# A decoder layer on one core: the token products in another order, the layer norm beside them, and the memory weights loaded from elsewhere

## The chip, the cores and the metric

The kernel runs on one core of a Trainium2 chip. A core has five engines that work side by side, each on a list of instructions of its own, in order: TensorE (PE in the profile; matmuls and transposes), VectorE (DVE), ScalarE (ACT), GpSimd (POOL) and SyncE (SP, which here only issues transfers). Semaphores tie the lists together. The on-chip memory SBUF feeds the engines, matmuls add up in the banks of PSUM, and 16 DMA engines move data to and from the chip's main memory. The metric is device time in microseconds (us) for one execution, less is better.

## The reference

One layer of a decoder for 1024 tokens of width 1024, in fp32: a gated FFN, a mixer of three branches, and a second FFN. The change lies in the mixer:

```python
h = rmsnorm(x, mix_norm[l])
z = h @ w_in[l]                       # u | v | c_q | c_kv | k_rope | q_mem | gates
u = gelu(z[..., COL_U:COL_V]); v = gelu(z[..., COL_V:COL_CQ])
y_a = spatial_gating(u, v, ...)       # u * (tril(W_s) layernorm(v) + b), 8 chunks of 128, 8 groups
y_b = mla(c_q, c_kv, k_rope, ...)     # low-rank q, k, v; norms; rotary; causal attention
y_c = memory_attention(q_mem, mem, ...)   # 4 heads, keys and values from 256 memory rows
merged = sum(sigmoid(gate_i) * (y_i @ w_branch_i))
x = x + merged @ w_out[l]
```

## The kernel before

Every fp32 product is computed as three matmuls on a rounded part and a rest (`mm3`: hi·hi, lo·hi, hi·lo). The two parts are made by `split`: ScalarE casts the rounded part, VectorE subtracts it to get the rest. Names that end in `hi` and `lo` are such pairs; `h`, `x`, `w`, `raw` are room of shared pools.

The kernel is one straight program. Who does what when is set in two ways: by the order in which the code is written, from which a scheduler makes one list for each engine, and by `after(i, first)` (L403), which holds instruction i behind another one in its engine's list and makes no semaphore wait of its own. Transfers take eight semaphores in turn, so an issue also waits until the transfer eight places before it has landed.

The stretch around the change, in the profile's time:

- **Token products** (`token_rows`, 988 to 1060 us): the columns of z that hold half of v and the low-rank latents of q, k and v are made for all tokens by a scheme of seven products (`b11`, `t2`, `b21`, `t1`, `t3`, `b22`, `t4`), each on halves of the rows, the inner width and the columns. Sums of products give half 0 (tokens 0 to 511) and half 1. `lat.norm` normalises a half's latents, `lat.turn` transposes them on TensorE. Here half 1 is done first.
- **q/k/v stage** (`qkv`, 1060 to 1110 on TensorE): four iterations of two tiles of 128 tokens, in the order 4, 6, 0, 2. TensorE multiplies, ScalarE copies out of PSUM (q L451, squares L452 and L462, k L463, v L464), VectorE sums and scales (L453 to L482), GpSimd rotates q (`rotate`, L358 to L363), and SyncE stores v, k and q to main memory (`vd` L467, `kd` L487, `qd` L490). Between iterations the generator `asides` does something else: the second turn, memory rows, and the layer norm of half 0.
- **Spatial gating and memory products** (`sgu`, 1110 to 1158): `mem_kv` makes keys and values from the memory rows in two products of 48 matmuls, with weights (`wkv`) that `mem_weights` loads as hi/lo pairs; `head_norm` normalises the keys (squares and copies L624, L625, reductions L626, product L630); `layer_norm` (statistics L551, L552, then L555 and L557) finishes v; `split(0)` and `split(1)` round its halves to `v_hi`, `v_lo` (L134, L135); a table load and a small `warm` activation (L603) prepare the later exponentials; `mix(0)` and `mix(1)` are the gating's matmuls, eight copies `u` each (L587), transposes (L593) and the product with u's transpose (L594), whose result `t` is split to `x`, the input of the first branch product. `branches` casts the branch weights from `raw` to `whi`, `wlo`. The tiles `v_hi` and `v_lo` lie in a pool of their own, in the room that q, k and v of the stage before have left, so their first writer waits for the last stores from there.
- After this come the branch products, memory attention and causal attention, the output product and the second FFN. The change doesn't touch these.

Of the kernel before, what the change touches and what calls it, by code (L numbers as in the profile page):

```python
# [8 lines left out]
F32 = mybir.dt.float32  # L9
F32R = mybir.dt.float32r  # L10
# [6 lines left out]
P = 128  # L17
D = 1024
# [31 lines left out]
class Kernel:  # L50
# [3 lines left out]
    def __init__(self, ctx, tc, a, out):  # L54
        self.tc, self.nc, self.a, self.out, self.last = tc, tc.nc, a, out, None
# [77 lines left out]
    def split(self, hi, lo, src, eng=None):  # L133
        self.nc.scalar.copy(hi, src)  # L134
        return (eng or self.nc.vector).tensor_tensor(lo, src, hi.bitcast(F32), op=ALU.subtract)  # L135
# [292 lines left out]
    def qkv(self, lat, asides):  # L428
# [8 lines left out]
        with tc.tile_pool(name="qkvp", bufs=2) as p:  # L437
            for i0 in (4, 6, 0, 2):
                q = p.tile([P, T, H, QK], F32, name="q")
# [3 lines left out]
                for t in range(T):  # L443
# [19 lines left out]
                    nc.scalar.copy(k[:, t, :, :NOPE], pv[:, :, :NOPE])  # L463
                    nc.scalar.copy(v[:, t], pv[:, :, NOPE:])  # L464
                    nc.vector.tensor_reduce(ss[:, 1, t], sq, axis=AXX, op=ALU.add)
                    nc.vector.tensor_scalar(ss[:, 1, t], ss[:, 1, t], krs[:, i:i + 1], None, op0=ALU.add)
                nc.sync.dma_start(self.vd[:, i0:i0 + T], v.rearrange("p t h d -> p t (h d)"))  # L467
                var = self.stat("qk_v", 2 * T * H)
                v4 = var.rearrange("p (a t h) -> p a t h", a=2, t=T)
                for t in range(T):  # L470
# [10 lines left out]
                    k[:, :, :, :NOPE], k[:, :, :, :NOPE], bk.to_broadcast([P, T, H, NOPE]), op=ALU.mult)  # L481
                nc.vector.tensor_tensor(  # L482
                    k[:, :, :, NOPE:], krr[:, i0:i0 + T].unsqueeze(2).to_broadcast([P, T, H, ROPE]),
# [4 lines left out]
                for t in range(T):  # L488
                    d = self.qd[:, :, i0 + t].rearrange("g p e -> p g e")
                    nc.sync.dma_start(d, q[:, t].rearrange("p (g x) d -> p g (x d)", x=2))  # L490
                next(asides, None)

# [51 lines left out]

    def layer_norm(self, v):

        nc = self.nc
        st = self.small.tile([P, 2, 6], F32, name="bn", tag="bn")
        mv = self.small.tile([P, 2, 2], F32, name="mv", tag="mv")
        for k in range(2):  # L550
            nc.vector.bn_stats(st[:, k], v[:, k])  # L551
            nc.vector.bn_aggr(mv[:, k], st[:, k])  # L552
        r = self.rms(mv[:, :, 1], 2, 1)
        for k in range(2):
            nc.vector.scalar_tensor_tensor(  # L555
                v[:, k], in0=v[:, k], scalar=mv[:, k, 0:1], in1=self.ln[:, 0], op0=ALU.subtract, op1=ALU.mult)
            nc.vector.scalar_tensor_tensor(  # L557
                v[:, k], in0=v[:, k], scalar=r[:, k:k + 1], in1=self.ln[:, 1], op0=ALU.mult, op1=ALU.add)

    def sgu(self, rows, p, sink):  # L560
        nc, a, tc = self.nc, self.a, self.tc
        v8 = lambda tag, dt=F32R: p.tile([P, 4, SGW], dt, name=tag, tag=tag, bufs=2)
        if True:
# [10 lines left out]
            def split(hf):  # L574
                vs[hf] = v8("v_hi"), v8("v_lo")
                for i, v in enumerate(rows[hf]):
                    self.split(*(x[:, 2 * i:2 * i + 2] for x in vs[hf]), v)

# [21 lines left out]
            for v in rows[1]:  # L600
                self.layer_norm(v)
            split(1)
            nc.scalar.activation(self.stat("warm", 1), vs[1][0][:, 3, SGW - 1:].bitcast(F32), ACT.Exp, scale=0.0)  # L603
            mix(0)
# [128 lines left out]
    def mem_kv(self, mt, w):  # L733


        nc, a = self.nc, self.a
        kt, vv = (tuple(self.h4(F32R) for _ in range(2)) for _ in range(2))
        kt = tuple(t.rearrange("p a (b m) -> p (a b) m", b=2) for t in kt)

        def product(w):  # L740
# [9 lines left out]
        self.head_norm(x, [ps[:, 0], ps[:, 1]])  # L750
        w = self.mem_weights(1, [None] * 4)
        yield
# [233 lines left out]
    def mixer(self, lat):  # L986
# [17 lines left out]
        with tc.tile_pool(name="lt", bufs=1) as p:  # L1004
            half = ROPE // 2
            for hf in (1, 0):
                t = slice(hf * 4, hf * 4 + 4)
# [504 lines left out]
class Gates(Seven):  # L1512
# [87 lines left out]
    def token_rows(self):  # L1600
# [41 lines left out]
        w = ready(S2)  # L1642
        p1, low = room(h4)
        for t in range(4):
            nc.scalar.copy(p1[t], a[t][:, :RW])
        lat.gain()
        product(x, w, "t2", True)
        w = ready(A12)
        both(A12, A12, S2, ALU.subtract)
        v1, _ = room(w4)  # L1650
        for t in range(4):
            tt(v1[t], p1[t], x[t][:, :RW], op=ALU.add)
        both(A21, A21, A22, ALU.add)
# [9 lines left out]
        v2, _ = room(w4)  # L1663
        for t in range(4):
            tt(v2[t], p1[t], x[t][:, :RW], op=ALU.add)
        lat.norm(1, high)
        y = [k.bank() for _ in range(4)]
        product(y, w, "t3", True)
        w = ready(A12)
        lat.v[0] = [h4() for _ in range(2)]  # L1670
# [12 lines left out]
        k.ln = h4()  # L1683
        for n, name in enumerate(("sg_ln_g", "sg_ln_b")):
            nc.sync.dma_start(k.ln[:, n], k.a[name].partition_broadcast(P))
        product(y, w, "t4", ps=(1,))
        for t in range(4):
            tt(v1[t], v1[t], y[t][:, :RW], op=ALU.add)
            gelu(1, t, v1[t], False)
        return lat  # L1690


class Latents:


    def __init__(self, k, src):
        self.k, self.src, self.v, self.xs = k, src, {}, {}
        self.krs, self.eps, self.cs = (k.const.tile([P, NT], F32, name=n) for n in ("krs", "eps", "cs"))
# [8 lines left out]
    def norm(self, half, ts):  # L1707
# [11 lines left out]
        for n, x in enumerate(xs):  # L1719
            nc.vector.scalar_tensor_tensor(  # L1720
                x[:, :KVR], in0=x[:, :KVR], scalar=r[:, n:n + 1], in1=self.g, op0=ALU.mult, op1=ALU.mult)
# [14 lines left out]
    def turn(self, half, bank=None):  # L1736

        k, xs = self.k, self.xs.pop(half)
        if half:
            self.ckv = [k.split_pair(k.h4) for _ in range(2)]  # L1740
            self.cq.append(k.split_pair(k.h4))
# [433 lines left out]
```

## Time and profile before

| | |
|---|---|
| median of 3 runs | 2191.41 us (2190.87 to 2194.07) |
| the profiled execution's own time | 2190.79 us |
| its span | 2189.1 us |
| granted clock of TensorE, mean | 0.996 |
| PE busy | 2164.3 us, 99% of the span |
| DVE, ACT, POOL busy | 72%, 42%, 13% |
| DMA | 329.97 MB, 151 GB/s over the span |

A share of 99% leaves some 25 us in which TensorE does nothing. The views that matter here are those that name a stretch: windows (busy time of every engine between two times), waits (what ended an engine's idle time) and the timeline (instructions one by one). A time is the distance from the span's start. A matmul's duration in the timeline overlaps the next one's; the distance of two starts is what it costs.

### The profile page before, as it was taken

Reading aid. Unit: us, or ns where it says so; the run is one execution under the profiler, and the core shown is the slowest. Engines: PE = TensorE matmul, PEld = TensorE weight load, DVE = VectorE, ACT = ScalarE, POOL = GpSimd, SP = SyncE. Lnnn points to the kernel's source line nnn. Section 1 sums busy time; section 2 is a strip of 40 time slices with the busy share of each in tenths; the row PEclk is TensorE's granted clock in tenths of the full one; section 3 lists DMA queues with packets and bytes.
Section 4 is the critical chain, followed back from the end, with each engine's and each line's share of the span. In section 5 each row is a group of like instructions: output and inputs, shape, how many; then the busy total and the mean of one; then the engine's idle time right before and its main releaser. Section 6 shows DMA issues by size and latency. Waiting matters only on the chain.

```text
span 2189.1 us, 27495 instructions
## 1 busy us (share of the span) xinstructions
PE 2164.3 (99%) x10154; PEld 1806.3 (83%) x10154; DVE 1583.6 (72%) x2389; ACT 915.2 (42%) x1500; POOL 275.4 (13%) x274
## 2 busy tenths in 40 slices
PE   9999999999999999999989999999999999999999
PEld 5888888888887888888968889988888888888887
DVE  7976666679889656755876679885886666667884
ACT  5433333343455434434545459833432322234332
POOL 2011111100000000000232321140011211210000
PEclk9999999999999999999989999999999999999999
DMA  4253444485432455542576631093033223338443
GB/s 146 92 192 139 146 140 144 151 308 169 134 118 97 144 173 178 198 137 92 173 269 232 247 147 59 13 347 142 29 137 98 102 97 102 115 124 294 169 130 106
DMA packets 125367, 329.97 MB, mean 151 GB/s; under 512 B 14768, under 2 KB 23088, under 8 KB 125232
## 3 DMA queue, kind: packets, MB, share of 16 engines
q1 hardware_dynamic: 125232, 328.21, 43.0%
q8 instruction: 80, 1.31, 0.2%
q14 instruction: 55, 0.45, 0.1%
HBM read 223.82 MB, written 104.33 MB: 150 GB/s over the span
## 4 chain that ended last, share of the span: by engine, by line
PE 90%; DVE 5%; ACT 2%; DMA 1%; issue 1%; POOL 1%; SPq 0%; ACTq 0%; POOLq 0%; DVEq 0%
PE one L151 15%; PE one L152 15%; PE one L153 15%; PE bank L151 13%; PE bank L152 12%; PE bank L153 12%; PE bank L926 1%; PE mm L151 1%; PE mm L152 1%; PE mm L153 1%; PE bank L941 1%; PE bank L942 1%; PE bank L421 1%; DVE wlo L140 1%; DMA kd<-k 0%
## 5 line engine op out<-in xcount | busy, mean ns | idle before, releaser
L139 ACT CAST whi<-x 128x1024 fp32r<-128x1024 f32 (+1 forms) x203 | 193.6, 955 | 444.8 <-PE one L152 168.5
L1337 DVE TENSOR_TENSOR t<-t,one 128x512 f32<-128x512 f32 x188 | 129.1, 687 | 212.2 <-PE one L153 212.1
L140 DVE TENSOR_TENSOR wlo<-x,whi 128x1024 fp32r<-128x1024 f32 (+1 forms) x203 | 246.5, 1215 | 35.4 <-ACT whi L139 25.8
L151 PE MATMUL bank<-h,whi 128*128 128x512 f32 x636 | 247.7, 390 | 0.0
L153 PE MATMUL bank<-h,wlo 128*128 128x512 f32 x636 | 247.5, 389 | 0.0
L152 PE MATMUL bank<-h,whi 128*128 128x512 f32 x636 | 247.4, 389 | 0.0
L151 PE MATMUL one<-h,whi 128*128 128x512 f32 x516 | 202.4, 392 | 0.0
L153 PE MATMUL one<-h,wlo 128*128 128x512 f32 x516 | 201.3, 390 | 0.0
L152 PE MATMUL one<-h,whi 128*128 128x512 f32 x516 | 201.2, 390 | 0.0
L151 PE MATMUL one<-w,whi 128*128 128x512 f32 x432 | 168.7, 391 | 0.0
L153 PE MATMUL one<-w,wlo 128*128 128x512 f32 x432 | 168.1, 389 | 0.0
L152 PE MATMUL one<-w,whi 128*128 128x512 f32 x432 | 168.1, 389 | 0.0
L135 DVE TENSOR_TENSOR wlo<-w,whi 128x1024 fp32r<-128x1024 f32 (+2 forms) x113 | 115.8, 1038 | 69.9 <-ACT whi L134 69.6
L134 ACT CAST whi<-w 128x1024 fp32r<-128x1024 f32 (+2 forms) x113 | 100.0, 902 | 152.9 <-PE one L152 63.3
L1915 POOL TENSOR_TENSOR raw<-raw 128x512 f32<-128x512 f32 x38 | 57.0, 1501 | 798.4 <-DVE raw L1770 711.7
L153 PEld LDWEIGHTS bank<-h,wlo 128*128 128x128 f32 x636 | 119.4, 188 | 24.9
L151 PEld LDWEIGHTS bank<-h,whi 128*128 128x128 f32 x636 | 119.4, 188 | 24.7
L152 PEld LDWEIGHTS bank<-h,whi 128*128 128x128 f32 x636 | 119.4, 188 | 24.5
L151 PE MATMUL bank<-whi 128*128 128x512 f32 x352 | 136.9, 389 | 0.0
L152 PE MATMUL bank<-wlo,whi 128*128 128x512 f32 x352 | 136.9, 389 | 0.0
L153 PE MATMUL bank<-whi,wlo 128*128 128x512 f32 x352 | 136.9, 389 | 0.0
L151 PEld LDWEIGHTS one<-h,whi 128*128 128x128 f32 x516 | 97.3, 189 | 20.2 <-issue 0.2
(393 smaller groups left out, 4925.6 us busy)
## 6 DMA issues: line engine op xcount, KB each, us to landing
x<-in_ffn_w_gu_dram SPq DMA_DIRECT2D x78, 512.0 KB, 5.0
w<-tdt SPq DMA_DIRECT2D x40, 512.0 KB, 4.5
gate<-raw SPq DMA_DIRECT2D x33, 512.0 KB, 2.9
tdb<-raw SPq DMA_DIRECT2D x64, 256.0 KB, 2.1
h<-in_ffn_w_down_dram SPq DMA_DIRECT2D x64, 256.0 KB, 6.0
w<-tdb SPq DMA_DIRECT2D x30, 512.0 KB, 4.5
tdt<-w SPq DMA_DIRECT2D x48, 256.0 KB, 2.1
x<-in_w_gate_dram SPq DMA_DIRECT2D x22, 512.0 KB, 6.7
```

Of the source, the lines that this page charges most:

```text
L134: self.nc.scalar.copy(hi, src)
L135: return (eng or self.nc.vector).tensor_tensor(lo, src, hi.bitcast(F32), op=ALU.subtract)
L139: self.nc.scalar.copy(hi, src)
L140: return lambda: self.nc.vector.tensor_tensor(lo, src, hi.bitcast(F32), op=ALU.subtract)
L151: i = mmul(out, s[0], m[0], start=first, stop=False, **kw)
L152: mmul(out, s[0], m[1], start=False, stop=False, **kw)
L153: self.last = mmul(out, s[1], m[0], start=False, stop=last, **kw)
L421: nc.tensor.transpose(b[:m, k * P:(k + 1) * P], s, self.ident)
L926: nc.tensor.transpose(b[:, at:at + P], prs[t][:, kk * P:(kk + 1) * P], self.ident)
L941: nc.tensor.matmul(o, w, pt[0], start=n == 0, stop=False)
L1337: return self.nc.vector.tensor_tensor(out, x, y, op=ALU.add)
L1915: sub = lambda d, x, y: (eng or nc.gpsimd).tensor_tensor(d, x, y, op=ALU.subtract)
```

## The change

Six things are different.

1. `token_rows` runs its products in the order b11, t2, t1, t3, b22, t4, b21. The last one is added to p1 by VectorE; four copies out of PSUM on ScalarE (L1659) are gone. Half 0's latents are done first, its transposes stand between the two parts of the last product, and `qkv` runs in the order 0, 2, 4, 6.
2. The layer norm of half 0 is at the end of `token_rows`; that of half 1 is put behind the k product of the second iteration (`qk_mark`).
3. The head norm's reductions are put behind the last `v_lo` of half 0 (`v_mark`).
4. The casts of the first branch's weights are put behind the `warm` activation (`hold`).
5. The second half of the memory weights is issued by ScalarE, behind its last copy of v (`vc_mark`), no longer by SyncE; of the first half's four pairs, three are loaded early into other room and one by SyncE behind v's third store (`vd_mark`).
6. Room for the memory keys and values is taken after the head norm.

```diff
     def split(self, hi, lo, src, eng=None):
-        self.nc.scalar.copy(hi, src)
+        i = self.nc.scalar.copy(hi, src)
+        if self.hold is not None:
+            self.after(i, self.hold)
         return (eng or self.nc.vector).tensor_tensor(lo, src, hi.bitcast(F32), op=ALU.subtract)
...
-            for i0 in (4, 6, 0, 2):
+            for i0 in range(0, NT, 2):
...
-                    nc.scalar.copy(v[:, t], pv[:, :, NOPE:])
+                    self.vc_mark = nc.scalar.copy(v[:, t], pv[:, :, NOPE:])
...
-                nc.sync.dma_start(self.vd[:, i0:i0 + T], v.rearrange("p t h d -> p t (h d)"))
+                i = nc.sync.dma_start(self.vd[:, i0:i0 + T], v.rearrange("p t h d -> p t (h d)"))
+                if i0 == 2 * T:
+                    self.vd_mark = i
...
+                if i0 == T:
+                    self.qk_mark = mark
...
-            nc.vector.bn_stats(st[:, k], v[:, k])
+            self.after(nc.vector.bn_stats(st[:, k], v[:, k]), mark)
...
-                    self.split(*(x[:, 2 * i:2 * i + 2] for x in vs[hf]), v)
+                    self.v_mark = self.split(*(x[:, 2 * i:2 * i + 2] for x in vs[hf]), v)
...
             for v in rows[1]:
-                self.layer_norm(v)
+                self.layer_norm(v, self.qk_mark)
             split(1)
-            nc.scalar.activation(self.stat("warm", 1), vs[1][0][:, 3, SGW - 1:].bitcast(F32), ACT.Exp, scale=0.0)
+            mark = nc.scalar.activation(self.stat("warm", 1), vs[1][0][:, 3, SGW - 1:].bitcast(F32), ACT.Exp, scale=0.0)
...
+            self.hold = mark
             next(branch)
+            self.hold = None
...
-            nc.vector.tensor_reduce(
+            i = nc.vector.tensor_reduce(
                 ss[:, k * MH:(k + 1) * MH], sq.rearrange("p (h d) -> p h d", d=MD), axis=AXX, op=ALU.add)
+            self.after(i, self.v_mark)
...
-        ps = product(w + self.mem_weights(0, [None] * 2, 2))
+        ps = product(w + self.mem_weights(0, [None], 3))
...
-                self.nc.sync.dma_start(t.bitcast(F32), src)
+                eng = self.nc.scalar if g else self.nc.sync
+                i = eng.dma_start(t.bitcast(F32), src)
+                if not room:
+                    self.after(i, self.vc_mark if g else self.vd_mark)
...
         def asides():
-            lat.turn(0)
-            self.mem_w = self.mem_weights(0, [self.split_pair] * 2)
+            lat.turn(1)
+            self.mem_t = self.mem_rows()
             yield
-            self.mem_t = self.mem_rows()
-            self.layer_norm(lat.v[0][0])
+            pair = lambda: self.split_pair(self.h4)
+            self.mem_w = self.mem_weights(0, [pair, pair, room])
             yield
-            self.layer_norm(lat.v[0][1])
-            yield
...
-        product(a, w, "b21")
-        w = ready(A21)
-        lat.v[1] = [h4() for _ in range(2)]
-        x1, high = room(h4, LW)
-        for t in range(4):
-            nc.scalar.copy(x1[t], a[t][:, :LW])
-            gelu(1, t, a[t][:, LW:RW], True)
         product(x, w, "t1")
...
-            tt(p1[t], p1[t], x[t][:, :RW], op=ALU.add)
-            gelu(0, t, p1[t][:, LW:], True)
+            tt(v2[t], p1[t], x[t][:, :RW], op=ALU.add)
+            gelu(0, t, v2[t][:, LW:], True)
         lat.load()
         lat.norm(0, low)
-        product(y, w, "t4", ps=(0,))
-        lat.turn(1, k.single)
...
-        product(y, w, "t4", ps=(1,))
+        product(y, w, "t4")
+        w = ready(A12)
+        lat.v[1] = [h4() for _ in range(2)]
         for t in range(4):
             tt(v1[t], v1[t], y[t][:, :RW], op=ALU.add)
             gelu(1, t, v1[t], False)
+        x = [k.single() for _ in range(4)]
+        product(x, w, "b21", True, (0,))
+        lat.turn(0)
+        product(x, w, "b21", True, (1,))
+        for t in range(4):
+            tt(p1[t], p1[t], x[t][:, :RW], op=ALU.add)
+            gelu(1, t, p1[t][:, LW:], True)
+        lat.norm(1, high)
+        for v in lat.v[0]:
+            k.layer_norm(v, lat.scaled[0])
```

How the lists change, at three places. VectorE, from the last k of the q/k/v stage to the rounding of v, before (`hn_ss` are the sums of the head norm, `rms_v` and `rs_y` its and the layer norm's roots; the rows between the first `rs_y` and L630 go on with the roots):

```order
L482 TENSOR_TENSOR k<-h_7670,rs_y 128x16x32
L626 TENSOR_REDUCE hn_ss<-t 128x4 x2
L135 TENSOR_TENSOR wlo<-raw,whi 128x512 x3
L180 TENSOR_SCALAR rms_v<-hn_ss 128x8
L180 TENSOR_SCALAR rms_v<-mv 128x2 x2
L135 TENSOR_TENSOR wlo<-raw,whi 128x512
L162 TENSOR_SCALAR rs_y<-rms_v 128x8
```

Up to here nothing of v is rounded. VectorE goes on, before, from the head norm's product to the first gating product:

```order
L630 TENSOR_TENSOR h_8927<-h_8927,rs_y 128x1024
L557 SCALAR_TENSOR_TENSOR h_7794<-h_7794,rs_y,h_8139 128x512 x2
L557 SCALAR_TENSOR_TENSOR h_7795<-h_7795,rs_y,h_8139 128x512 x2
L135 TENSOR_TENSOR v_lo<-h_7967,v_hi 128x1024
L135 TENSOR_TENSOR v_lo<-h_7968,v_hi 128x1024
L135 TENSOR_TENSOR v_lo<-h_7794,v_hi 128x1024
L135 TENSOR_TENSOR v_lo<-h_7795,v_hi 128x1024
L594 TENSOR_TENSOR t<-t,bank 128x512 x4
```

All four `v_lo` stand together here, behind the layer norm. The same place of the changed kernel (L137 is the old L135, L486 the old L482, L634 the old L626, L563 the old L557, L600 the old L594):

```order
L486 TENSOR_TENSOR k<-h_7670,rs_y 128x16x32
L137 TENSOR_TENSOR v_lo<-h_7863,v_hi 128x1024
L137 TENSOR_TENSOR v_lo<-h_7864,v_hi 128x1024
L634 TENSOR_REDUCE hn_ss<-t 128x4 x2
L182 TENSOR_SCALAR rms_v<-hn_ss 128x8
```

Two `v_lo` now stand ahead of the sums. VectorE goes on, in the changed kernel, again from the head norm's product:

```order
L639 TENSOR_TENSOR h_8925<-h_8925,rs_y 128x1024
L563 SCALAR_TENSOR_TENSOR h_8040<-h_8040,rs_y,h_7672 128x512 x2
L563 SCALAR_TENSOR_TENSOR h_8041<-h_8041,rs_y,h_7672 128x512 x2
L600 TENSOR_TENSOR t<-t,bank 128x512 x4
L137 TENSOR_TENSOR v_lo<-h_8040,v_hi 128x1024
L137 TENSOR_TENSOR v_lo<-h_8041,v_hi 128x1024
L137 TENSOR_TENSOR x_9027<-t,x_9026 128x512
```

The `v_lo` of half 0 moved ahead of the head norm and the layer norm, the `v_lo` of half 1 behind the first gating product, and the branch weights (`wlo<-raw`) behind all of these.

ScalarE, around its casts of v, before:

```order
L625 COPY h_8927<-mm 128x512
L134 CAST whi<-raw 128x512 x4
L134 CAST v_hi<-h_7967 128x1024
L134 CAST v_hi<-h_7968 128x1024
L134 CAST v_hi<-h_7794 128x1024
L134 CAST v_hi<-h_7795 128x1024
L603 ACT_TABLE_LOAD
L603 ACTIVATE warm<-v_hi 128x1
L587 ACTIVATE u<-bank,c_sg_b 128x4x64 x8
```

Branch weights go first here, then all of v. And now, from the end of its eight loads of memory weights (not shown, between the last copy of v and these rows):

```order
L633 COPY h_8925<-mm 128x512
L134 CAST v_hi<-h_7863 128x1024
L134 CAST v_hi<-h_7864 128x1024
L593 ACTIVATE u<-bank,c_sg_b 128x4x64 x8
L134 CAST v_hi<-h_8040 128x1024
L134 CAST v_hi<-h_8041 128x1024
L134 CAST x_9026<-t 128x512
L609 ACT_TABLE_LOAD
L609 ACTIVATE warm<-v_hi 128x1
L134 CAST whi<-raw 128x512 x2
L145 ACTIVATE h_8950<-bank,c_mem_k_norm 128x512
L134 CAST whi<-raw 128x512 x2
```

The four casts of branch weights moved from ahead of v to behind the warm-up, and half 1's v and the table load behind the eight `u` of the first mixing.

SyncE, the end of the q/k/v stage, before (`kd`, `qd`, `vd` are the stores of k, q and v, `mq` the memory queries):

```order
L467 DMA vd<-v 128x1024
L768 DMA wlo<-wkv 128x1024
L768 DMA whi<-wkv 128x1024
L590 DMA t<-gate_3314 128x512
L590 DMA t<-gate_3315 128x512
L590 DMA t<-gate_3316 128x512
L590 DMA t<-gate_3317 128x512
L487 DMA kd<-k 128x4x192 x2
L590 DMA t<-gate_3314 128x512
L590 DMA t<-gate_3315 128x512
L100 DMA raw<-in_w_branch_dram 128x1024
L490 DMA qd<-q 128x4x192 x2
```

The last store of q is the last row. The same place of SyncE's list now:

```order
L469 DMA vd<-v 128x1024
L494 DMA qd<-q 128x4x192 x2
L596 DMA t<-gate_3314 128x512
L596 DMA t<-gate_3315 128x512
L596 DMA t<-gate_3316 128x512
L596 DMA t<-gate_3317 128x512
L491 DMA kd<-k 128x4x192 x2
L494 DMA qd<-q 128x4x192 x2
L596 DMA t<-gate_3314 128x512
L596 DMA t<-gate_3315 128x512
L789 DMA v_hi<-mq 128x1024 x2
```

The memory weights left this part of SyncE's list, the last store of q comes two gates and a branch weight earlier, and the branch weights stand behind the memory queries.

## Rows read from the trace of the kernel before

**Rows 1.** The page's first line.

```profile
span 2189.1 us, 27495 instructions
```

**Rows 2.** Windows by stage: length; busy time of each engine; clock, DMA share, GB/s.

```profile
987.70:1059.60 71.90, 71.90 (x349) 64.28 (x348) 42.35 (x86) 31.61 (x92) 2.58 (x5) 1.00 0.35 111
1059.60:1109.94 50.34, 49.11 (x254) 44.37 (x252) 45.76 (x109) 29.09 (x62) 17.35 (x24) 1.00 0.56 188
1109.94:1158.28 48.34, 37.83 (x185) 31.66 (x184) 38.60 (x81) 22.16 (x42) 13.24 (x12) 0.86 0.82 302
1160.00:1280.00 120.00, 119.16 (x660) 103.27 (x658) 70.78 (x125) 46.95 (x130) 39.22 (x32) 1.00 0.65 241
```

**Rows 3.** Waits of TensorE, 1055 to 1160: us in total, times, longest.

```profile
PE bank L151 <- ACT v_hi L134: 7.0, 1, 7.0
PE mm L151 <- DMA whi<-wkv: 1.8, 1, 1.8
```

**Rows 4.** Timeline of ScalarE: start, us, instruction, [idle before, what ended it].

```profile
1117.86 0.60 ACT L464 COPY v<-mm 128x512 f32<-128x512 f32 x1
...
1122.93 2.21 ACT L134 CAST whi<-raw 128x512 fp32r<-128x512 f32 x4
1140.50 3.89 ACT L134 CAST v_hi<-h 128x1024 fp32r<-128x1024 f32 x4 [15.36 <-DMA raw<-in_w_branch_dram]
1144.41 1.28 ACT L603 ACT_TABLE_LOAD   x1
...
1150.31 1.23 ACT L134 CAST x<-t 128x512 fp32r<-128x512 f32 x2 [0.68 <-DVE t L594]
1151.43 0.69 ACT L143 ACTIVATE h<-bank,c_mem_k_norm 128x512 fp32r<-128x512 f32 x1
...
1153.46 1.02 ACT L134 CAST h<-mm 128x1024 fp32r<-128x1024 f32 x1
...
1155.23 2.34 ACT L587 ACTIVATE u<-bank,c_sg_b 128x256 f32<-128x256 f32 x6
```

**Rows 5.** Timeline of TensorE, from the first mixing to the first branch matmul.

```profile
1142.59 1.20 PE L151 MATMUL bank<-v_hi,x 128*128 128x256 f32 x4 [7.01 <-ACT v_hi L134]
...
1156.38 0.28 PE L152 MATMUL bank<-v_lo,x 128*128 128x256 f32 x1
1156.50 0.28 PE L153 MATMUL bank<-v_hi,x 128*128 128x256 f32 x1
...
1158.28 0.48 PE L151 MATMUL bank<-x,whi 128*128 128x512 f32 x1
```

**Rows 6.** Timeline of SyncE: the last issue of q's stores.

```profile
1132.32 1.02 SPq L490 DMA_DIRECT2D qd<-q  x2
```

**Rows 7.** The line that stores q, 1080 to 1145: from issue to landing.

```profile
DMA to landing us min/median/max: 2.7/5.4/8.6
```

**Rows 8.** Timeline of GpSimd: the last step of the last rotation.

```profile
1128.42 1.17 POOL L363 TENSOR_TENSOR q<-rot,rot 128x256 f32<-128x256 f32 x1
```

**Rows 9.** The window of full DMA, columns as in rows 2.

```profile
1105.60:1139.90 34.30, 28.14 (x119) 22.75 (x117) 29.37 (x79) 9.54 (x20) 13.24 (x12) 0.93 1.03 378
```

**Rows 10.** DMA issues, 1085 to 1160: count, KB each, median us to landing.

```profile
whi<-wkv SPq DMA_DIRECT2D x6, 512.0 KB, 8.1
```

**Rows 11.** Timeline of VectorE, from the head norm's reductions to the first gating product.

```profile
1124.78 1.27 DVE L626 TENSOR_REDUCE hn_ss<-t 128x4 f32<-128x512 f32 x2
...
1128.93 0.69 DVE L180 TENSOR_SCALAR rms_v<-hn_ss 128x8 f32<-128x8 f32 x1
...
1132.24 1.21 DVE L630 TENSOR_TENSOR h<-h,rs_y 128x1024 f32<-128x1024 f32 x1
1133.37 2.73 DVE L557 SCALAR_TENSOR_TENSOR h<-h,rs_y,h 128x512 f32<-128x512 f32 x4
1141.58 4.63 DVE L135 TENSOR_TENSOR v_lo<-h,v_hi 128x1024 fp32r<-128x1024 f32 x4 [5.48 <-ACT v_hi L134]
1149.59 2.48 DVE L594 TENSOR_TENSOR t<-t,bank 128x512 f32<-128x512 f32 x4 [3.37 <-PE bank L593]
```

More of the change, by code (lines that the diff above doesn't have):

```diff
@@ L54, in __init__ @@
     def __init__(self, ctx, tc, a, out):
-        self.tc, self.nc, self.a, self.out, self.last = tc, tc.nc, a, out, None
+        self.tc, self.nc, self.a, self.out, self.last, self.hold = tc, tc.nc, a, out, None, None
         pool = lambda name, bufs=1, **k: ctx.enter_context(tc.tile_pool(name=name, bufs=bufs, **k))
@@ L481, in qkv @@
                     k[:, :, :, :NOPE], k[:, :, :, :NOPE], bk.to_broadcast([P, T, H, NOPE]), op=ALU.mult)
-                nc.vector.tensor_tensor(
+                mark = nc.vector.tensor_tensor(
                     k[:, :, :, NOPE:], krr[:, i0:i0 + T].unsqueeze(2).to_broadcast([P, T, H, ROPE]),
@@ L543, in branch, with layer_norm @@
             self.mm3(ps, wb[j], tuple(x[:, hf * 512:hf * 512 + 512] for x in yt[j]), j == 0, j == 3)
-    def layer_norm(self, v):
+    def layer_norm(self, v, mark):
         nc = self.nc
@@ L736, in mem_kv @@
         nc, a = self.nc, self.a
-        kt, vv = (tuple(self.h4(F32R) for _ in range(2)) for _ in range(2))
-        kt = tuple(t.rearrange("p a (b m) -> p (a b) m", b=2) for t in kt)
         def product(w):
@@ L746, in product @@
             return ps
-        ps = product(w + self.mem_weights(0, [None] * 2, 2))
+        ps = product(w + self.mem_weights(0, [None], 3))
         x = self.h4().rearrange("p a (h d) -> p a h d", h=MH)
         self.head_norm(x, [ps[:, 0], ps[:, 1]])
+        kt, vv = (tuple(self.h4(F32R) for _ in range(2)) for _ in range(2))
+        kt = tuple(t.rearrange("p a (b m) -> p (a b) m", b=2) for t in kt)
         w = self.mem_weights(1, [None] * 4)
@@ L994, in asides @@
         def asides():
-            lat.turn(0)
-            self.mem_w = self.mem_weights(0, [self.split_pair] * 2)
+            lat.turn(1)
+            self.mem_t = self.mem_rows()
             yield
-            self.mem_t = self.mem_rows()
-            self.layer_norm(lat.v[0][0])
-            yield
-            self.layer_norm(lat.v[0][1])
+            pair = lambda: self.split_pair(self.h4)
+            self.mem_w = self.mem_weights(0, [pair, pair, room])
             yield
         with tc.tile_pool(name="lt", bufs=1) as p:
+            room = lambda: tuple(p.tile([P, D], F32R, name=n) for n in ("whi2", "wlo2"))
             half = ROPE // 2
-            for hf in (1, 0):
+            for hf in range(2):
                 t = slice(hf * 4, hf * 4 + 4)
@@ L1642, in token_rows @@
         w = ready(S2)
-        p1, low = room(h4)
+        p1, high = room(h4)
         for t in range(4):
@@ L1646, in token_rows @@
         lat.gain()
+        k.ln = h4()
+        for n, name in enumerate(("sg_ln_g", "sg_ln_b")):
+            nc.sync.dma_start(k.ln[:, n], k.a[name].partition_broadcast(P))
         product(x, w, "t2", True)
-        w = ready(A12)
-        both(A12, A12, S2, ALU.subtract)
+        both(A21, A21, A22, ALU.add)
+        w = ready(A21)
+        both(S2, A12, S2, ALU.subtract)
         v1, _ = room(w4)
@@ L1652, in token_rows @@
             tt(v1[t], p1[t], x[t][:, :RW], op=ALU.add)
-        both(A21, A21, A22, ALU.add)
-        product(a, w, "b21")
-        w = ready(A21)
-        lat.v[1] = [h4() for _ in range(2)]
-        x1, high = room(h4, LW)
-        for t in range(4):
-            nc.scalar.copy(x1[t], a[t][:, :LW])
-            gelu(1, t, a[t][:, LW:RW], True)
         product(x, w, "t1")
         w = ready(A11)
-        v2, _ = room(w4)
+        v2, low = room(w4)
         for t in range(4):
             tt(v2[t], p1[t], x[t][:, :RW], op=ALU.add)
-        lat.norm(1, high)
         y = [k.bank() for _ in range(4)]
         product(y, w, "t3", True)
-        w = ready(A12)
+        w = ready(S2)
         lat.v[0] = [h4() for _ in range(2)]
@@ L1676, in token_rows @@
         for t in range(4):
-            tt(p1[t], p1[t], x[t][:, :RW], op=ALU.add)
-            gelu(0, t, p1[t][:, LW:], True)
+            tt(v2[t], p1[t], x[t][:, :RW], op=ALU.add)
+            gelu(0, t, v2[t][:, LW:], True)
         lat.load()
         lat.norm(0, low)
-        product(y, w, "t4", ps=(0,))
-        lat.turn(1, k.single)
-        k.ln = h4()
-        for n, name in enumerate(("sg_ln_g", "sg_ln_b")):
-            nc.sync.dma_start(k.ln[:, n], k.a[name].partition_broadcast(P))
-        product(y, w, "t4", ps=(1,))
+        product(y, w, "t4")
+        w = ready(A12)
+        lat.v[1] = [h4() for _ in range(2)]
         for t in range(4):
@@ L1696, in __init__ @@
     def __init__(self, k, src):
-        self.k, self.src, self.v, self.xs = k, src, {}, {}
+        self.k, self.src, self.v, self.xs, self.scaled = k, src, {}, {}, {}
         self.krs, self.eps, self.cs = (k.const.tile([P, NT], F32, name=n) for n in ("krs", "eps", "cs"))
@@ L1719, in norm @@
         for n, x in enumerate(xs):
-            nc.vector.scalar_tensor_tensor(
+            self.scaled[half] = nc.vector.scalar_tensor_tensor(
                 x[:, :KVR], in0=x[:, :KVR], scalar=r[:, n:n + 1], in1=self.g, op0=ALU.mult, op1=ALU.mult)
@@ L1738, in turn @@
         k, xs = self.k, self.xs.pop(half)
-        if half:
-            self.ckv = [k.split_pair(k.h4) for _ in range(2)]
+        if half == 0:
+            self.ckv = [k.split_pair() for _ in range(2)]
             self.cq.append(k.split_pair(k.h4))
```

## The prediction

> **What bounds the kernel now.** Around the span of 2189.1 us [rows 1] lie 1.7 us more: the profiled execution took 2190.79. I read the windows next, because the change touches only the stretch from the token products to the first branch product. TensorE is the bound nearly everywhere: busy 71.90 of 71.90 us in the token products, 49.11 of 50.34 in the q/k/v stage, 119.16 of 120 after 1160 [rows 2], so work that is taken off other engines there is worth nothing. The hole is from 1109.94 to 1158.28: 37.83 busy of 48.34 us, at a granted clock of 0.86. That is 10.5 us idle, and about 5.3 us (14% of 37.83, my estimate) lost because part of the matmuls ran at the lower of the clock's two levels, 1.2 GHz, after the idle time. With the 1.2 us idle in the q/k/v stage, some 17 us is the most that the change can give back: 2190.8 - 17 = 2173.8 is a floor.
>
> Then the waits of TensorE: 7.0 us for the rounding of v (`v_hi`), 1.8 for a memory weight [rows 3]. The timelines tell where the long one comes from: the first `v_hi` cast starts at 1140.50 after ScalarE sat idle 15.36 us [rows 4], the first matmul that reads it at 1142.59, and the first branch matmul at 1158.28 [rows 5]. Call 1140.50 V0 and 1158.28 B; B - V0 is 17.8 us. The view puts ScalarE's wait down to a load of branch weights, but `v_hi` doesn't read these. Its room was q's and k's, so it waits for their last stores: SyncE issues the last pair of `qd` at 1132.32 [rows 6], and such a store lands 2.7 to 8.6 us after its issue [rows 7]; 1140.5 lies in that. Why so late: GpSimd ends the last rotation at 1129.6 [rows 8], SyncE still has gates and a branch weight ahead, and from 1105.6 to 1139.9 the DMA engines are full (share 1.03, 378 GB/s), with memory weights above all: six `whi` of 512 KB and as many `wlo` [rows 9, 10]. VectorE meanwhile does the head norm, branch-weight subtractions and the layer norm until 1136.1, and then waits too [rows 11].
>
> So B is set by V0, that is by the transfers, and by the chain behind V0. The change acts on both, in opposite directions.
>
> **The change part by part.**
>
> *Token products reordered (A).* The number of matmuls is the same; four ScalarE copies go. ScalarE is busy 31.61 and VectorE 42.35 of 71.90 us [rows 2], so neither is the bound, and TensorE has no idle time there to win. The transposes of one half stand in the middle of the last product, as they did. Half 0's layer norm goes to the end of this stage, half 1's behind the k of the second iteration. The cover is TensorE's last product; where it fails (its additions and the second half's latents come late, before the next stage reads them) a us or so is lost. I take 0, from -0.5 to +1.5. The q/k/v matmuls start where they did.
>
> *Memory weights elsewhere (B).* Of 16 loads of 512 KB, six come early, two go on SyncE behind v's third store, and the eight of the second half are issued by ScalarE behind its last v copy. That ended at 1118.5 [rows 4] and comes a little earlier, since VectorE has two layer-norm passes fewer in that stage: I take 1117. On SyncE a branch weight and two of six gates no longer stand before the last `qd`. What must move between 1117 and the landing of that `qd`, by the order of the two queues: 8 x 0.524 = 4.19 MB of weights, v's last store 0.52, two pairs of `qd` 1.57, the last `kd` 0.79, four gates 1.05: 8.1 MB, at 378 GB/s [rows 9] 21.5 us, so 1138.5, and with a us for the last to complete 1139.5. That these come in one heap is not only a matter of bandwidth. Transfers take eight semaphores in turn, and by the order the last two `qd` get those of the seventh and eighth weight load: SyncE waits for these to land. Weights, v, one pair of `qd` and some of the gates are 5.5 MB or more, 14.6 us, so 1131.6 to 1133, and a store of 5.4, the median [rows 7], lands at 1137 to 1138.5. Between the two ways I take 1138.5: V0 moves by **-2.0**. Bounds: if there is no heap, the rotation's end (1129.6 [rows 8], less 1.2) and a store of 2.7 us [rows 7] give 1131 to 1132, -8.5; if SyncE waits until 1133 and the store takes the longest, 8.6, with a us for SyncE's own issue, +2.
>
> What one queue does when another is full no row of before shows, since SyncE issued every transfer in this stretch. The Trainium skill (DMA: Bandwidth & Descriptors, section "Queues, rings and completion order") says that each DMA engine takes turns between the queues that have work, packet by packet, and (section "Issuing engines are not separate DMA queues") that issuing from several engines saves only issue time. By the first, SyncE's stores would not stand behind ScalarE's weights but share with them, which by itself would bring V0 to the end of -8.5; by the second the sum of bytes stays, and with it the 1138.5.
>
> *Ties and their order (C).* Before, all that VectorE did between its last k and `v_lo` (reductions, rms chain, head norm, layer norm) was done in the wait before V0. In the new order it stands **behind** the two `v_lo` of half 0, so none of it can start before V0, and half 1's v is rounded only after it. From V0 on VectorE [rows 11]: the first two `v_lo` begin after 1.1 and take 2.3 (half of 4.63), 3.4; reductions 1.3, 4.7; rms chain 3.3 (1128.93 to 1132.24), 8.0; head norm 1.1, 9.1; layer norm 2.7, 11.8. Meanwhile TensorE does the first mixing, as before. Then ScalarE, which works in order [rows 4]: two `v_hi` of half 1 (half of 3.89) 13.8; a cast of x 0.6, 14.4; table load and warm-up 1.4, 15.8; the four branch-weight casts, which the hold keeps behind the warm-up, 2.2, 18.0; two scalings of memory keys 1.2, 19.2; three casts of x 1.8, 21.0; the memory values 1.0, 22.0; eight `u` of the second mixing 8 x 0.39 = 3.1, 25.1. From the last `u` to the first branch matmul it was 0.7 [rows 4, 5]: 25.8 instead of 17.8, so +8.0. VectorE is no later: its first gating pass 2.5 and the last `v_lo` 2.3 end at 16.6. Less ten score matmuls that now run in this gap, 10 x 0.12 [rows 5] = 1.2, and less 0.4, since ScalarE's instructions overlap by some 0.05: **+6.4**. Bounds: +1, if V0 is no longer what the chain counts from, so that its work finds waits again to lie in; +8.5 without the two credits and with a little more.
>
> *After B (D).* The branch weights' loads start some 12 us later and their casts fall just ahead of their use. 119.16 of 120 us are busy after 1160 [rows 2], so nothing is to be won there; a stall of 0 to 3 us is possible. I take 0.
>
> *Sum* against the profiled execution (the median of the runs, 2191.41, is 0.6 above it): 0 - 2.0 + 6.4 + 0 = +4.4, **2195.2 us**.
>
> **The rivals.**
>
> 1. *Faster: the stores no longer stand behind weights.* If `qd` lands as soon as the rotation allows, V0 moves by -8.5, and if the chain behind it costs only its lower bound of +1, the sum is -7.5: 2183.3. For it: 6.3 MB of weights went through SyncE ahead of those stores [rows 10], and a head norm behind `v_lo` costs nothing where V0 is early enough to come before the head norm's input. Against: the eight loads start together just before these stores, and the semaphores.
> 2. *A wash.* V0 comes half of the way to its bound (-5) and the chain costs 5 to 6: about 2191.3. This also holds the case that the change of order does not reach the path at all.
> 3. *Much slower: what is issued behind the weights becomes the last.* ScalarE's loads keep the DMA engines until 1134, and last stores, gates, memory queries and branch weights all land later than their readers want them: V0 +2, the chain +8.5, a stall after B of 3, together +13.5: 2204.3. It decides from the point where the branch weights land later than 16 us behind V0, which is when their casts are due. Against: after V0 the DMA engines have little left to do.
>
> **How the numbers follow.** Forecast 0.42 (own range 2192.5 to 2199), faster 0.24, wash 0.23, much slower 0.11. About 0.2% (4.4 us) is what a measurement of this kernel can tell from no change: below 2187.0 is faster, above 2195.8 slower. The forecast's case lies half above that line and half below it, all of rival 3 above, rival 1 below 2187 but for a little, the wash between but for a little on either side: faster 0.26, same 0.39, slower 0.35. The range that leaves out 2 in 10 goes from 2182 (rival 1 at its price) to 2201.
>
> **What would show it.** Step B: the first `v_hi` cast between 1136 and 1142, with SyncE waiting for weights before its last `qd`; a start by 1133 shows half of rival 1. Step C: in VectorE's row the reductions of the head norm after `v_lo`, and 22 to 26 us from the first `v_hi` cast to the first branch matmul; under 19 makes the forecast wrong. Step A: no wait of TensorE over 1 us before 1109. Step D: over 3 us idle after the first branch matmul speaks for rival 3. The hole's idle time (10.5 us now) should be some 14 us, at a granted clock of 0.86 or below.

## The result, and the profile after

The changed kernel takes **2199.59 us** (median of 6 runs, 2199.12 to 2199.70) against 2191.32 for the kernel before (6 runs beside it): ratio 1.0037, 95% interval 1.0024 to 1.0050, so 8.3 us slower. The forecast was 2195.2, with a range of 2182 to 2201. The profiled execution has a span of 2197.8 us, 8.7 more than before, and the working below is made against that.

Windows of the changed kernel, columns as in [rows 2] (length, then busy time of PE, PEld, DVE, ACT and POOL, where PEld is TensorE's loading of its weights; clock, DMA share, GB/s):

```profile
987.70:1059.60 71.90, 71.90 (x350) 64.26 (x349) 43.84 (x77) 28.33 (x66) 3.85 (x10) 1.00 0.30 99
...
1109.94:1166.00 56.06, 40.21 (x179) 32.08 (x178) 36.59 (x86) 24.26 (x45) 11.08 (x12) 0.85 0.75 267
...
1111.00:1117.00 6.00, 5.46 (x24) 4.24 (x23) 5.88 (x9) 1.60 (x4) 2.82 (x3) 1.00 0.40 155
1117.00:1143.00 26.00, 18.17 (x75) 13.39 (x73) 8.24 (x17) 4.16 (x8) 8.26 (x10) 0.99 0.97 343
1142.50:1167.60 25.10, 17.12 (x88) 15.24 (x89) 22.36 (x58) 18.75 (x34) 0.00 (x0) 0.66 0.60 218
1167.60:1287.60 120.00, 119.96 (x663) 103.90 (x662) 70.68 (x125) 48.02 (x132) 39.16 (x32) 1.00 0.64 235
```

The token products are as full as before, and so is what follows the hole. The hole itself is where the time went: ahead of 1117 the DMA engines are at 0.40 and 155 GB/s, where before they ran at 378 from 1105.6 [rows 9]; from 1117 they are full; and from the first rounding of v to a us before the first branch matmul VectorE is busy 22.36 and ScalarE 18.75 of 25.10 us while TensorE works at a granted clock of 0.66.

ScalarE in the changed kernel (`ACTq` are its issues of loads; a row with x4 stands for four instructions in a row):

```profile
1118.21 0.60 ACT L466 COPY v<-mm 128x512 f32<-128x512 f32 x1
...
1127.21 0.33 ACTq L777 DMA_DIRECT2D wlo<-wkv  x1
1127.58 0.60 ACT L632 ACTIVATE t<-mm 128x512 f32<-128x512 f32 x1 [8.77 <-DMA whi<-wkv]
...
1142.45 1.99 ACT L134 CAST v_hi<-h 128x1024 fp32r<-128x1024 f32 x2 [12.82 <-DMA qd<-q]
1146.79 1.75 ACT L593 ACTIVATE u<-bank,c_sg_b 128x256 f32<-128x256 f32 x4 [2.34 <-PE bank L155]
...
1151.87 1.04 ACT L134 CAST v_hi<-h 128x1024 fp32r<-128x1024 f32 x1 [1.18 <-DVE h L563]
...
1154.78 1.28 ACT L609 ACT_TABLE_LOAD   x1
...
1156.18 1.12 ACT L134 CAST whi<-raw 128x512 fp32r<-128x512 f32 x2
...
1162.57 1.47 ACT L593 ACTIVATE u<-bank,c_sg_b 128x256 f32<-128x256 f32 x3
```

The first `v_hi` cast (V0) is at 1142.45 instead of 1140.50, and now the view itself names the last store of q. Half 1's cast comes 9.4 us behind it, because of what VectorE has to do between:

```profile
1143.53 2.36 DVE L137 TENSOR_TENSOR v_lo<-h,v_hi 128x1024 fp32r<-128x1024 f32 x2 [17.53 <-ACT v_hi L134]
1145.81 1.27 DVE L634 TENSOR_REDUCE hn_ss<-t 128x4 f32<-128x512 f32 x2
...
1149.30 1.21 DVE L639 TENSOR_TENSOR h<-h,rs_y 128x1024 f32<-128x1024 f32 x1
1150.43 2.73 DVE L563 SCALAR_TENSOR_TENSOR h<-h,rs_y,h 128x512 f32<-128x512 f32 x4
1153.08 2.47 DVE L600 TENSOR_TENSOR t<-t,bank 128x512 f32<-128x512 f32 x4
1155.48 2.35 DVE L137 TENSOR_TENSOR v_lo<-h,v_hi 128x1024 fp32r<-128x1024 f32 x2
```

VectorE sits idle 17.5 us with the sums, the head norm and the layer norm behind the `v_lo` that it waits for; before, it did them in that time [rows 11]. TensorE's first matmul of either place:

```profile
1144.55 1.20 PE L153 MATMUL bank<-v_hi,x 128*128 128x256 f32 x4 [6.85 <-ACT v_hi L134]
...
1168.74 0.48 PE L153 MATMUL bank<-x,whi 128*128 128x512 f32 x1
```

Why V0 was late, from the chain of the changed kernel, that is the work that ended last, each piece released by the one before it (start, us, piece):

```profile
1122.32 13.15 DMA qd<-q
1135.55 0.37 SPq L491
...
1136.73 0.72 SPq L494
1137.50 4.78 DMA qd<-q
1142.45 1.05 ACT v_hi L134
```

The third iteration's store of q takes 13.15 us to land. SyncE waits for it (its semaphore comes round again) before it issues the last `kd` (L491) at 1135.55 and the last `qd` (L494) at 1136.73, though the rotation ended at 1129.5. Ahead of that its gates (L596) waited in the same way, mostly for stores too; waits of SyncE, 1117 to 1145 (us in total, times, longest):

```profile
SPq L596 <- DMA vd<-v: 4.1, 1, 4.1
SPq L596 <- DMA qd<-q: 3.3, 1, 3.3
SPq L491 <- DMA qd<-q: 2.3, 1, 2.3
...
SPq L596 <- DMA wlo<-wkv: 1.6, 1, 1.6
```

What moved from 1117 to 1142.3, where the last `qd` had landed:

```profile
DMA packets 6097, 8.92 MB, mean 353 GB/s; under 512 B 336, under 2 KB 4432, under 8 KB 6096
```

Measured from the start Q of the q/k/v stage (its first matmul), so that what varies ahead of it drops out. B is the first branch matmul, the last column is what follows it:

| run | change | median us | V0 - Q | B - V0 | B - Q | span - B |
|---|---|---|---|---|---|---|
| before | | 2191.3 to 2192.2 | 80.9 | 17.8 | 98.7 | 1030.8 |
| after | all | 2199.59 | 82.3 | 26.3 | 108.6 | 1029.1 |
| x1 | after, no head-norm tie | 2197.68 | 84.7 | 21.3 | 106.0 | 1030.2 |
| x2 | after, no tie, no hold | 2197.65 | 86.3 | 17.3 | 103.6 | 1030.7 |
| x5 | x2, weights on SyncE | 2192.53 | 81.6 | 16.7 | 98.3 | 1030.2 |
| x10 | after, weights on SyncE | 2198.29 | 79.2 | 26.8 | 105.9 | 1029.1 |
| x3 | before, head-norm tie | 2195.24 | 80.8 | 26.4 | 107.1 | 1028.1 |
| x9 | before, weights on ScalarE | 2194.50 | 84.0 | 18.3 | 102.4 | 1030.3 |
| x4 | after, own room | 2194.48 | 69.4 | 31.7 | 101.1 | 1030.3 |
| x6 | after, gates behind `qd` | 2198.39 | 80.0 | 26.2 | 106.1 | 1029.0 |
| x7 | x4 and x6 | 2190.74 | 69.4 | 29.2 | 98.6 | 1030.4 |
| x8 | before, gates behind `qd` | 2188.25 | 77.0 | 18.3 | 95.3 | 1030.9 |
| x11 | x5, x4 and x6 | 2187.29 | 70.3 | 24.2 | 94.5 | 1030.3 |

The four right columns are of one profiled execution each; runs of one kernel spread by some 4 us, so a profile can lie a few us beside its median (x3's is the slowest of its eleven runs and lies 3.3 above).

### The profile page after: what moved, and what is told of

Read it like the earlier page. It is cut to its first block, busy times and chain, and to the rows that moved or that the text cites. A ratio compares the mean times of both kernels' runs of the same rounds, so it can differ in the third digit from the quotient of the medians.

```text
span 2197.8 us, 27491 instructions
## 1 busy us (share of the span) xinstructions
PE 2166.6 (99%) x10154; PEld 1807.2 (82%) x10154; DVE 1581.6 (72%) x2393; ACT 913.8 (42%) x1496; POOL 270.2 (12%) x274
## 3 DMA queue, kind: packets, MB, share of 16 engines
q10 hardware_dynamic: 1152, 4.19, 0.5%
## 4 chain that ended last, share of the span: by engine, by line
PE 89%; DVE 5%; ACT 2%; DMA 1%; issue 1%; POOL 1%; SPq 0%; ACTq 0%; POOLq 0%; DVEq 0%
PE one L153 15%; PE one L154 15%; PE one L155 15%; PE bank L153 12%; PE bank L154 12%; PE bank L155 12%; PE bank L937 1%; PE mm L153 1%; PE mm L154 1%; PE mm L155 1%; DMA qd<-q 1%; PE bank L952 1%; PE bank L953 1%; PE bank L423 1%; DVE wlo L142 1%
## 5 line engine op out<-in xcount | busy, mean ns | idle before, releaser
L137 DVE TENSOR_TENSOR wlo<-w,whi 128x1024 fp32r<-128x1024 f32 (+2 forms) x112 | 114.7, 1037 | 67.2 <-ACT whi L134 67.0
```

## The experiments

The theory: two parts of the change each lengthen one side of V0, the head norm's tie the chain behind it, the weights' move to ScalarE the transfers ahead of it. The rivals: only one of them does; or the token order does. Comments in the code cuts are not in the code.

**x1 and x2: without the ties.**

```diff
-            self.after(i, self.v_mark)      # x1 and x2
-            self.hold = mark                # x2
```

> The changed kernel without the tie that puts the head norm's reductions behind v's first rounding; all else as changed. By the chain theory (the tie puts 8 us of VectorE's work behind the first v_hi cast): the head norm and layer norm run again before V0, V0 stays near 1143, V0 to the first branch matmul falls from 26.3 to about 20 us (17.8 as before plus 2.2 for the branch-weight casts that are still held), so about 2195 us. If the transfers alone cost the 8 us: no change, 2199 to 2200. If the tie alone cost them all: 2191.

> The changed kernel without the head norm's tie and without the hold on the branch weights. Chain theory: V0 to the first branch matmul is back at about 18 us, V0 itself stays late (1142 to 1144, from 1140.5) because the memory weights still come late on ScalarE's queue: 2192.5 to 2194. If the weights' move costs nothing: 2191 or less. If the ties are not the cause: 2199.

Ratios to before 1.0028 (1.0017 to 1.0039) and 1.0025 (1.0015 to 1.0034). The chain did what the theory said, 21.3 and 17.3 us, but the times did not: V0 went to 84.7 and 86.3 us behind Q. In both lists the last store of q falls behind two more gates, in x2 behind a branch weight too; that the scheduler places them earlier because VectorE's work comes earlier is likely and not shown. The chain of x2:

```profile
1138.88 0.19 SPq L596
1139.17 1.00 SPq L596
1140.26 0.43 SPq L100
1140.79 0.38 SPq L494
1141.23 6.79 DMA qd<-q
1148.23 3.89 ACT v_hi L134 x4
```

So the ties are not all of it: with none of them V0 is 5.4 us later than before.

**x3: the tie alone, in the kernel before.**

```diff
-            nc.vector.tensor_reduce(
+            i = nc.vector.tensor_reduce(
...
+            self.after(i, self.v_mark)      # v_mark set in split(), as in the change
```

> The kernel before with one part of the change alone: the head norm's reductions behind v's first rounding. Chain theory: V0 as before (1140 to 1141), V0 to the first branch matmul 23 to 25 us instead of 17.8 (26.3 less the 2.2 of casts that are not held here), so 2196 to 2198 us. If the tie is harmless by itself and the late weights are the cause: 2191.

1.0014 (1.0005 to 1.0022), 3.4 us: V0 where it was, the chain 26.4, a little over the 23 to 25 that were expected. The tie is bad by itself; in the median by a little less than expected, and by less than its profile shows.

**x4: room that doesn't wait for the stores of q and k.**

```diff
-        with tc.tile_pool(name="qkvp", bufs=2) as p:
+        with tc.tile_pool(name="qkvx", bufs=1) as px, tc.tile_pool(name="qkvp", bufs=2) as p:
...                                           # v, sq and rotate's tiles from px
-        with tc.tile_pool(name="sgu", bufs=1) as p:
+        with tc.tile_pool(name="sg0", bufs=1) as p0, tc.tile_pool(name="sgu", bufs=1) as p:
...                                           # v_hi, v_lo of half 0 from p0, of half 1 from p
```

> The changed kernel with q and k in a pool of their own and v's first half rounded into the room of the other tiles, so that its first cast no longer waits for the last stores of q and k (v's second half still does). If V0 is set by these stores: the first v_hi cast starts at about 1130, behind the head norm's copies and the last rotation, 12 us earlier. What comes late next should be the second half's cast (stores, 1142) and then the branch weights (loaded behind the memory queries): first branch matmul at 1160 to 1166, 2191 to 2197 us. If something else than the stores held the cast: V0 at 1142 and 2199.

1.0011 (1.0002 to 1.0020). That V0 is set by those stores is shown: with the room changed and nothing else it starts 13 us earlier, and the second half, which still lies in q's and k's room, where the first was.

```profile
1129.83 2.03 ACT L134 CAST v_hi<-h 128x1024 fp32r<-128x1024 f32 x2
1142.73 1.99 ACT L134 CAST v_hi<-h 128x1024 fp32r<-128x1024 f32 x2 [10.87 <-DMA qd<-q]
1144.62 1.56 ACT L594 ACTIVATE u<-bank,c_sg_b 128x256 f32<-128x256 f32 x4
```

The gating's copies `u` stand behind the second cast in ScalarE's list, so 5.4 of the 13 us are given back (B - V0 is 31.7 instead of 26.3).

**x5: the weights on SyncE again.**

```diff
-                eng = self.nc.scalar if g else self.nc.sync
+                eng = self.nc.sync
...
-                    self.after(i, self.vc_mark if g else self.vd_mark)
+                    self.after(i, self.vd_mark)
```

> The changed kernel without the head norm's tie and the hold (as x2), and with the second half's memory weights issued by SyncE again, as early as room allows, instead of by ScalarE behind its last v copy. What is left of the change: the order of the token products, the layer norm's places, and three early pairs of weights. If the move to ScalarE's queue is what made V0 late in x2 (5.4 us later than before, counted from the start of the q/k/v stage): V0 back at 80 to 82 us behind that start and 2190.5 to 2192.5 us. If the token order or the layer norm cost the rest: 2195 or more.

1.0004 (0.9995 to 1.0014): no difference from before. So the order of the token products, the layer norm's places and the three early pairs together are worth nothing that shows, and the weights' move is what x2 loses. That move is two things at once, though: another queue, and a later start. ScalarE issues its eight loads from 1117.3 on in the changed kernel, SyncE issues them from 1109.5 on in x5. The same six us as above, in x5:

```profile
1111.00:1117.00 6.00, 5.47 (x24) 4.50 (x25) 5.84 (x10) 1.35 (x4) 3.16 (x3) 1.00 1.02 378
```

From 45 to 57 us behind Q 1.59 MB are moved in x2 and 2.92 in x5; at 378 GB/s the difference is 3.5 us (an estimate), and V0 differs by 4.7. So the late start by itself may be most of it. A run with the loads on SyncE but as late, or on ScalarE but as early, would tell the two apart; there is none. Stores of q, issue to landing, 1115 to 1145, in x5:

```profile
DMA to landing us min/median/max: 7.4/7.8/8.1
```

and in the changed kernel:

```profile
DMA to landing us min/median/max: 4.5/8.6/13.1
```

**x6 and x8: gates behind the last store of q**, in the kernel after and before.

```diff
-                    nc.sync.dma_start(d, q[:, t].rearrange("p (g x) d -> p g (x d)", x=2))
+                    self.qd_mark = nc.sync.dma_start(d, q[:, t].rearrange("p (g x) d -> p g (x d)", x=2))
...
-                    nc.sync.dma_start(u, self.z[ZU + j][:, hf])
+                    self.after(nc.sync.dma_start(u, self.z[ZU + j][:, hf]), self.qd_mark)
```

> The changed kernel with one edit: the gate rows that SyncE loads for the mixing stand behind the last store of q, not ahead of the last stores of k and q. If SyncE's list and its semaphores made the last stores late (the last pair of qd issued at 1136.7, though the rotation ended at 1129.5): qd issued by 1131, the first v_hi cast 5 to 7 us earlier (75 to 77 us behind the start of the q/k/v stage), the chain behind it unchanged at 26 us: 2192.5 to 2194.5. If the heap of bytes set it whatever the order: V0 within 1.5 us of the changed kernel's and 2198 to 2200.

> The kernel before with the edit of x6 alone: six gate loads, 1.57 MB or 4.1 us at 378 GB/s, no longer stand ahead of the last stores of k and q. If V0 is set by those stores before as after: V0 76 to 78 us behind the start of the q/k/v stage (80.9 before), the chain behind it unchanged at 17.8: 2187 to 2189. If the stores were bound by bytes of the memory weights or the gates are then late for the gating product: 2190 to 2193.

In the kernel before it does what was expected: V0 3.9 us earlier, 2188.25, ratio 0.9984 (0.9975 to 0.9993). In the changed kernel (2198.39, 1.0029, 1.0018 to 1.0041) V0 gains 2.4 instead of 5 to 7, and the time is that of the second case. Its chain tells why:

```profile
1121.03 12.56 DMA qd<-q
1133.66 0.36 SPq L494
1134.06 6.90 DMA qd<-q
1141.27 1.05 ACT v_hi L134
```

The issue of the last `qd` waits for the third iteration's store, which again takes 12.6 us beside ScalarE's loads. Order on SyncE is one part; the heap of transfers that are in flight at once is, by this chain, the other.

**x7: own room and gates together.**

> x4 (v's first half rounded into room that doesn't wait for the stores of q and k) together with the edit of x6. The second half's cast, which in x4 waited for the stores until 82.3 us behind the start of the q/k/v stage, should start at 75 to 77, and the first branch matmul 5 to 6 us before x4's: 2188 to 2190 us. If something else comes last (ScalarE's casts, the memory weights): 2191.5 to 2194.5, as x4.

0.9996 (0.9988 to 1.0005), 0.7 us above the expected range: the second half's cast starts 79.8 us behind Q, not 75 to 77, and B is 2.5 us before x4's, not 5 to 6.

**x9 and x10: one part each**, x9 the weights' move alone in the kernel before, x10 the changed kernel with x5's edit and both ties.

> The kernel before with the other suspected part alone: the second half's memory weights issued by ScalarE behind its last v copy; no ties, token order and first half's weights as before. If that move by itself makes V0 late (x2 against x5: 86.3 against 81.6 us behind the start of the q/k/v stage, 5.1 us of the median): V0 at 85 to 87 and 2195.5 to 2197.5 us. If it needs the early loads or the new token order: 2191 to 2193.

> The changed kernel with both ties kept, only the second half's memory weights on SyncE again, early. x3 gave 3.4 us for the head norm's tie alone in the kernel before. If tie and weights act one by one: V0 80 to 82 us behind the start of the q/k/v stage, the chain behind it 26, and 2194.5 to 2197 us, that is 2.5 to 5 us less than the changed kernel. If with the ties the weights' queue no longer matters: 2198 to 2200.

x9 1.0013 (1.0005 to 1.0022): V0 84.0, the same direction as x2, a little less. x10 1.0025 (1.0014 to 1.0035): V0 a little earlier than expected, the chain as expected, the median 1.3 above the range and in that of the second case: with the ties in place the weights' move costs 1.3 us in the median, and the intervals of the two ratios overlap. With x2, x5 and the changed kernel this is a table of two by two: no ties, weights on SyncE 2192.5; weights on ScalarE 2197.7; ties 2198.3; both 2199.6. Alone they cost 5.1 and 5.8 us, together 7.1. They are not additive; a part of that is that with the ties the last `qd` stands ahead of two gates and a branch weight (V0 - Q is 82.3 in the changed kernel, 86.3 in x2).

**x11: what the runs speak for, in one** (x5, x4's room, x6's order).

> The parts that the runs so far speak for, in one: no ties, memory weights on SyncE, gate loads behind the last store of q (x8), and v's first half in room that doesn't wait for these stores (x4). Two gains that don't lie behind one another would give: second half's cast at 77 us behind the start of the q/k/v stage as in x8, first mixing done before it, first branch matmul 3 to 5 us before x8's 95.3: 2184 to 2186.5 us. If ScalarE's list (the second half's cast stands ahead of the first mixing's copies) eats the early start: 2187 to 2189, as x8.

2187.29 us, 0.9977 (0.9968 to 0.9986), 4.9 us faster than the kernel before, clear of noise; no clear difference from x8. The second of the two cases came: TensorE's largest wait in that stretch is

```profile
PE bank L153 <- ACT u L594: 5.6, 3, 4.2
```

the gating's copies behind half 1's cast.

## Why the prediction was right, and where it was off

The direction was right, and so was the mechanism in its main part, the tie's chain behind V0; the size was 4 us too small. By the terms of the sum, against the profiled execution (+8.7):

- **A** (token order, layer norm), taken as 0: Q moved by 0.5, within what Q varies from profile to profile (1059.3 to 1062.0), and x5 has the same time as before. Right. One wait of TensorE before 1109 took 1.2 us, a little over the 1 us of the sign.
- **B** (V0), taken as -2.0 with a bound of +2: +1.4 behind Q, or +1.95 from the span's start. This is the step that failed. The prediction had two ways to V0. By bytes: the sum left out the third iteration's two `kd` stores, 0.79 MB issued at 1116.3 and 1116.7, which moved after 1117 as well: 8.92 MB instead of 8.1, or 2.1 us at 378 GB/s. The rate was 353 GB/s instead of 378, another 1.7 us. Together 21.5 + 2.1 + 1.7 = 25.3 us, so 1142.3. By the wait: the last two `qd` did get the semaphores of the seventh and eighth weight load, but these had landed at 1133.3 and 1134.9 (by the last counts of their semaphores in the trace); what SyncE stood for until 1135.5 was the third iteration's store of q, which took 13.15 us where each store was given the median of 5.4. The end of -8.5, where stores would gain from a second queue, did not come: in x9 V0 is 3.1 us later than before, in x2 4.7 later than in x5. These runs start the loads later as well, so they don't show what the queue alone does.
- **C** (the chain), +8.0 gross, less 1.6: measured 26.3 - 17.8 = 8.5, less 1.8 that the stretch behind B is shorter (1030.8 to 1029.1). x3 and x10 give 26.4 and 26.8 for the same tie elsewhere. The cause is right: VectorE's work stands behind the tie and holds up half 1's cast. That the number is as close is in part luck, since two errors cancel. By the list of the prediction the memory values end 22.0 us behind V0; they ended at 18.5, since the sums and roots took 1.1 us less, the first of half 1's casts did not wait for the whole layer norm, and two casts of x came later. From there to B the prediction had 3.8 us, as ScalarE's work alone; it took 7.8. There TensorE's granted clock was 0.50, the lower of its two levels, behind two waits of 1.9 us each (up to 1153.8 and 1157.9), and its gating matmuls start 0.21 us apart, where they start 0.12 apart before [rows 5]; three of the last copies `u` waited for them. The memory values on ScalarE, two rows of TensorE, and the window:

```profile
1159.92 1.00 ACT L134 CAST h<-mm 128x1024 fp32r<-128x1024 f32 x1
...
1164.60 0.41 PE L154 MATMUL bank<-v_lo,x 128*128 128x256 f32 x1
1164.81 0.41 PE L155 MATMUL bank<-v_hi,x 128*128 128x256 f32 x1
...
1157.00:1165.50 8.50, 5.86 (x24) 5.27 (x24) 8.09 (x12) 7.61 (x16) 0.00 (x0) 0.50 0.69 240
```

- **D** (after B), 0: 119.96 of 120 us busy. Right.

0.5 + 1.4 + 8.5 - 1.8 = 8.6. Of the rivals, the much slower one had both V0 (+2) and the chain (+8.5) right; its stall of 3 after B did not come, and 1.8 came back there instead. So the measured time lies midway between the forecast and that rival, and V0 (1142.45, for 1136 to 1142) and B - V0 (26.3, for 22 to 26) lie just outside what was to show the forecast.

## What to carry to other kernels

A tie that puts work behind an instruction pays only when that instruction is early; first find what the instruction itself waits for, because in the wait before it the work was free. What an early tile waits for may be the last user of its room, not its data: x4 moved a cast by 13 us by changing rooms alone, and the time by 5.1. And when transfers bound a stretch, look at what stands ahead of the one that is waited for: moving six gate loads behind it (x8) was the one single edit that beat the kernel before, by 3.9 us. In the changed kernel the same edit (x6) gained 1.2: there the store ahead of it was the longer wait.

## What the runs showed of the hardware

Two queues at work at once did not get equal parts of the DMA engines. From 1117 to 1135 in the changed kernel (queue, packets, MB, share of 16 engines' time; q10 is ScalarE's, q1 SyncE's):

```profile
q10 hardware_dynamic: 1152, 4.19, 61.5%
q1 hardware_dynamic: 2344, 2.29, 39.6%
```

ScalarE's loads go in packets of some 3640 bytes (4.19 MB by 1152), SyncE's stores and gates in packets of 977 on average, and ScalarE's queue moved 65% of the bytes. A 384 KB store took 13.15 and 12.56 us from issue to landing beside these loads (changed kernel, x6), at most 8.1 with the same weights on the one queue (x5), where they also start earlier and stand ahead of the stores. A load of 512 KB on ScalarE's queue took 5.3 to 10.2 us in the changed kernel. The Trainium skill (DMA: Bandwidth & Descriptors, section "Queues, rings and completion order") says that a DMA engine takes turns between queues by packet; the trace agrees with that in so far as the queue with small packets got the smaller part of the bytes, but whether the profile's packets are the page's is not shown, and the runs don't separate packet size, the number of transfers in flight and the loads' later start from one another. In the prediction that rule stood for an earlier store; the measurement is the other way.

An engine that issues loads also waits for their semaphores: ScalarE could do nothing from 1118.8 to 1127.6 (8.77 us, the row of L632) while its eight loads took their turns. In x10, where SyncE issues them, the same instruction L632 starts 63.0 us behind Q, here 67.4, so some 4.5 us of that were the issues. They cost nothing here, because what ScalarE does next stands ahead of the wait for the stores.
